# Softmax scaling of all four row blocks on VectorE instead of three shared between VectorE and GpSimd

## The chip, the cores and the metric

The kernel runs on one core of a Trainium2 chip, as one program. The metric is device time in microseconds, from the first to the last instruction of one launch. Of 3 runs of the kernel before, the median is 1939.57 us (1939.19 to 1943.88).

## The reference

Two transformer blocks follow each other on one sequence of 512 tokens and 1024 channels, all in fp32. What matters here are the two dense softmaxes over 512 keys. The first block has a causal attention with 8 heads, the second a window attention and a selected-block attention with 16 heads each; at 512 tokens both of the latter see every earlier key, so that each is a causal softmax too, weighted with a gate per head and row:

```python
sc = jnp.where(k_idx[None, :] <= q_idx[:, None], sc, -jnp.inf)
pr = jax.nn.softmax(sc, axis=-1)                    # first block, 8 heads
...
p_s = jax.nn.softmax(logit_s, axis=-1)              # second block, 16 heads
p_w = jax.nn.softmax(logit_w, axis=-1)              # second block, 16 heads
o = gt[..., 0:1] * o_c + gt[..., 1:2] * o_s + gt[..., 2:3] * o_w
```

That makes 8 softmax tables in the first attention and 32 in the second. The rest are matrix products (input projections, gated feed-forward layers), a depthwise convolution of width 31 beside the first attention, and norms.

## The kernel before

Activations lie transposed, 128 channels to a tile of 512 tokens. Each matrix product is made of three TensorE products of a high and a low part (lines 305 to 307), so every weight and activation is split: ScalarE casts the high part (lines 280 and 286), and VectorE, for some tiles GpSimd, subtracts it for the low part (lines 281 and 287).

A softmax table (`softmax`, from line 484) has four row blocks i = 3, 2, 1, 0 with 512, 384, 256 and 128 allowed keys, side by side in one tile `pw`. For each block TensorE makes the scores (line 500), VectorE adds the bias table and takes the row's minimum into `nm` (line 506), ScalarE takes the exponential and the row sum `rs` (line 508). After two blocks VectorE takes the two reciprocals into `cf` (line 510), and then both blocks are scaled in place by `cf` and by the gate (line 512): a number in the first attention, a column of `gcol` in the second. The pair (3, 2) is scaled by GpSimd, the pair (1, 0) by VectorE. Then `weigh1` and `weigh` transpose the scaled blocks on TensorE (lines 718 and 525), copy or split them (lines 721, 286 and 287) and multiply them with the values (lines 723 and 533); the first transposes of a table with `first` set need all four blocks, those of the other form begin with blocks 2 and 3.

In the first attention VectorE also has the taps of the convolution for two of its four channel tiles (line 610, 512 columns each), GpSimd those of the others (line 608), and GpSimd makes the low parts of keys and queries (lines 287 and 793). In the second attention GpSimd also subtracts the bias table from the mask (`tb`, line 1324), multiplies weights by a norm's gain (line 276) and makes low parts of queries, attention outputs and output weights (lines 287 and 281); VectorE adds the output projection into x (line 1318).

The program is written as one stream. A list scheduler decides at build time in which order the instructions stand on each engine; each engine then goes through its own list in that order, and waits for semaphores where an operand isn't ready. Conv taps and output projections are given a lower priority, so the scheduler uses them as filling.

Of the kernel before, what the change touches and what calls it, by code (L numbers as in the profile page):

```python
# [10 lines left out]
OP = mybir.AluOpType  # L11
# [203 lines left out]
def _body(tc, A, out):  # L215
    nc = tc.nc
    V, S, P, G = nc.vector, nc.scalar, nc.tensor, nc.gpsimd
# [27 lines left out]
    def bank(tag):  # L245
        return ps[0].tile([128, T], FT, name=tag, bufs=banks[tag])
# [238 lines left out]
    def softmax(pl, passes, tab, gate, bufs):  # L485

        nm = pl.tile([128, 4], FT, name="nm", bufs=bufs)
        rs = pl.tile([128, 4], FT, name="rs", bufs=bufs)
        c = pl.tile([128, 4], FT, name="cf", bufs=bufs)
        w = [None] * 4  # L490
        pw = pl.tile([128, 1280], FT, name="pw", bufs=bufs)
        off = 0
        for i in (3, 2, 1, 0):
            n = 128 * (i + 1)
            if i:
                s = bank("s")
                for i_ in (1, 0) if i == 1 else (i,):
                    s_ = s[:, :128 * (i_ + 1)] if i_ else s[:, 256:384]
                    for j, (a, b) in enumerate(passes):
                        P.matmul(s_, a[:, 128 * i_:128 * i_ + 128], b[:, :128 * (i_ + 1)],  # L500
                                 start=j == 0, stop=j == len(passes) - 1)
            else:
                s = s[:, 256:384]
            w[i] = t = pw[:, off:off + n]
            off += n
            V.tensor_tensor_reduce(out=t, in0=s[:, :n], in1=tab[:, 384 - 128 * i:], op0=OP.add, op1=OP.min,  # L506
                                   scale=1.0, scalar=3.0e38, accum_out=nm[:, i:i + 1])
            S.activation(t, t, AF.Exp, bias=nm[:, i:i + 1], scale=-1.0, accum_out=rs[:, i:i + 1])  # L508
            if i % 2 == 0:
                V.reciprocal(c[:, i:i + 2], rs[:, i:i + 2])  # L510
                for k in (i + 1, i):
                    (G if i else V).tensor_scalar(w[k], w[k], c[:, k:k + 1], gate(k), op0=OP.mult, op1=OP.mult)  # L512
        return w

    def weigh(pl, w, vst, o, first, last):
# [181 lines left out]
    for i in range(4):  # L697
        acc = bank("mm")
        for k in range(2):
            s = slice(128 * i, 128 * i + 128)  # L700
            w = slice(512 * k, 512 * k + 512)
# [63 lines left out]
    for hp in range(MH // 2):  # L765
# [15 lines left out]
        for par in range(2):  # L781
            h = 2 * hp + par
            if h == 6:
                conv_norm(0)
            uq = unit(A["w_q_b"][h])
            acc = bank("mm")
            mm(acc, uq, qa)
            qf = at.tile([128, T], FT, name="qf", bufs=1)
            begin = V.tensor_tensor(qf, acc, tq[par], op=OP.mult)
            qh = at.tile([128, T], FR, name="qh", bufs=2)  # L790
            ql = at.tile([128, T], FR, name="ql", bufs=2)
            S.copy(qh, qf)
            (G if h > 1 else V).tensor_tensor(ql, qf, qh, op=OP.subtract)
            with tc.issue_after(begin.ins):
                conv_taps(3, range(SPREAD[h], SPREAD[h + 1]))
            kh, kl = ka[par]
            if h > 5:
                start_out(h - 6)
            w = softmax(at, ((qh, kh), (qh, kl), (ql, kh)), mask, lambda k: 1.0, 3)
            weigh1(w, lambda j: vt[:, j, hp, 64 * par:64 * par + 128], o, par)  # L800
# [91 lines left out]
    for ch in range(3):  # L892
        hid = []
        for f in range(8 * ch, min(8 * ch + 8, FT1)):
# [6 lines left out]
            for k in range(2):  # L901
                V.scalar_tensor_tensor(y, gpad[:, k:k + T], col("ffn_dw_w", 3 * f + k), y,
                                       op0=OP.mult, op1=OP.add)
# [79 lines left out]
    for c in range(KT):  # L983
# [10 lines left out]
        for k in range(2):  # L994
            V.scalar_tensor_tensor(y, gpad[:, k:k + T], col("a_conv_w", 3 * c + k), y,
                                   op0=OP.mult, op1=OP.add)
# [262 lines left out]
    for g in range(4):  # L1259
        d = acc[:, 64 * g:64 * g + 64]  # L1260
        for k in range(2):
            sh, sl = [z[:, k, 128 * g:128 * g + 128] for z in hv]
            w = slice(64 * k, 64 * k + 64)
# [56 lines left out]
    def head(g, j, of):  # L1320
        h = 4 * g + j
        tb = aw.tile([128, T], FT, name="tb", bufs=2)
        nc.sync.dma_start(tb, A["bias"][h])
        G.tensor_tensor(tb, mask, tb, op=OP.subtract)
        o = bank("o")
        place = PLACE[4 * g + j]

        def blocks(n):
            if n == place:
                for e_ in range(2):  # L1330
                    P.matmul(o, vz[:, g, j, :], pcs[g][e_], start=n == 0 and e_ == 0, stop=n == 2 and e_ == 1)

        for b in range(2):
            blocks(b)
            k = kk[g][b]
            w = softmax(aw, ((qs[g][j], k[0]), (qs[g][j], k[1])), tb,
                        lambda i: gcol[:, i, 3 * h + 1 + b:3 * h + 2 + b], 3)
            weigh(aw, w, lambda jt: vt[g][:, jt, b, :], o, b == 0 and place > 0, b == 1 and place < 2)
        blocks(2)
        if h < NH - 1:  # L1340
            fold(aw, o, of, j % 2)
        return o
# [88 lines left out]
```

## Time and profile before

| what | value |
|---|---|
| profiled execution | 1939.04 us, span 1937.2 us |
| TensorE busy | 1858.0 us, 96% of the span |
| VectorE busy | 1295.1 us, 67% |
| ScalarE busy | 956.5 us, 49% |
| GpSimd busy | 412.0 us, 21% |
| TensorE granted clock, mean | 0.983 |

Busy time is a union of the instructions' spans on an engine. Consecutive instructions on VectorE overlap by a few hundredths of a microsecond in the records, so what one costs its queue is the distance from its start to the next start. The first attention's softmaxes run at about 130 to 180 us of the span, the second's at about 1299 to 1540 us; all other stages have no instruction of line 512.

### The profile page before, as it was taken

To read this page: it belongs to the slowest core of one execution; us is meant where nothing else is said; L and a number is where in the kernel's file an instruction comes from. 1 tells how busy PE (TensorE), PEld (TensorE's weight loads), DVE (VectorE), ACT (ScalarE), POOL (GpSimd) and SP (SyncE) were. 2 spreads that over 40 slices of the span, in tenths; PEclk is the share of its full clock that TensorE was granted. 3 is DMA by queue.
4 is the path that set the end of the run, shared out by engine and by line. 5 is a ranking of instruction groups with operands and counts; after the bars stand their busy time and mean duration, and the time that the engine had idled before them with its cause. 6 is when DMAs were issued, how large, how long until landed. Compare 5 with 4: busy or idle time off the path is not lost. (4 is left out here: it accounts for less than half of the span.)

```text
span 1937.2 us, 27654 instructions
## 1 busy us (share of the span) xinstructions
PE 1858.0 (96%) x10198; PEld 1585.8 (82%) x10198; DVE 1295.1 (67%) x2294; ACT 956.5 (49%) x1755; POOL 412.0 (21%) x397
## 2 busy tenths in 40 slices
PE   8989999999999999999999999989999989999997
PEld 6767888888888878878888888778888878898886
DVE  7888566255355864486666666869887977666664
ACT  6686544233234432254444444646665755444443
POOL 2994230000003300010000002336454420000001
PEclk9989989999999999999999999999999989999998
DMA  4221323332322223334455542354232134555542
GB/s 150 81 75 31 100 75 97 98 98 88 98 93 93 77 87 98 118 93 135 130 131 139 142 131 77 111 149 124 78 90 80 36 93 134 148 130 137 136 115 76
DMA packets 82742, 202.11 MB, mean 104 GB/s; under 512 B 9904, under 2 KB 18288, under 8 KB 82608
## 3 DMA queue, kind: packets, MB, share of 16 engines
q1 hardware_dynamic: 77744, 184.88, 31.4%
q0 software_dynamic: 4032, 14.68, 4.5%
q8 instruction: 80, 1.31, 0.3%
q10 hardware_dynamic: 832, 0.79, 0.1%
q14 instruction: 54, 0.44, 0.1%
HBM read 187.73 MB, written 2.10 MB: 98 GB/s over the span
## 5 line engine op out<-in xcount | busy, mean ns | idle before, releaser
L280 ACT CAST whi<-raw 128x512 fp32r<-128x512 f32 (+4 forms) x342 | 260.8, 770 | 454.3 <-PE mm L306 345.8
L281 DVE TENSOR_TENSOR wlo<-raw,whi 128x512 fp32r<-128x512 f32 (+4 forms) x318 | 298.6, 945 | 115.4 <-ACT whi L280 110.7
L305 PE MATMUL mm<-hidh,whi 128*128 128x512 f32 (+1 forms) x794 | 295.3, 379 | 5.6 <-ACT hidh L286 5.0
L306 PE MATMUL mm<-hidl,whi 128*128 128x512 f32 (+1 forms) x794 | 300.4, 379 | 0.0
L307 PE MATMUL mm<-hidh,wlo 128*128 128x512 f32 (+1 forms) x794 | 297.9, 379 | 1.6 <-DVE wlo L281 1.6
L306 PE MATMUL mm<-xgl,whi 128*128 128x512 f32 (+1 forms) x608 | 231.7, 382 | 3.8 <-DVE xgl L290 1.9
L307 PE MATMUL mm<-xgh,wlo 128*128 128x512 f32 (+1 forms) x608 | 232.4, 383 | 0.4 <-DVE wlo L281 0.4
L305 PE MATMUL mm<-xgh,whi 128*128 128x512 f32 (+1 forms) x608 | 231.4, 383 | 0.7 <-ACT whi L280 0.7
L305 PEld LDWEIGHTS mm<-hidh,whi 128*128 128x128 f32 x794 | 148.9, 188 | 32.8 <-ACT hidh L286 5.4
L307 PEld LDWEIGHTS mm<-hidh,wlo 128*128 128x128 f32 x794 | 149.4, 188 | 29.5 <-DVE wlo L281 1.8
L306 PEld LDWEIGHTS mm<-hidl,whi 128*128 128x128 f32 x794 | 149.8, 189 | 27.1 <-DVE hidl L287 0.6
L344 POOL DMA_DIRECT2D raw<-mlp1f x28 | 24.6, 879 | 549.0 <-DMA raw<-mlp1f 273.8
L306 PEld LDWEIGHTS mm<-xgl,whi 128*128 128x128 f32 x608 | 115.4, 190 | 29.0 <-DVE xgl L290 3.0
L307 PEld LDWEIGHTS mm<-xgh,wlo 128*128 128x128 f32 x608 | 115.5, 190 | 22.8 <-DVE wlo L281 0.8
L305 PEld LDWEIGHTS mm<-xgh,whi 128*128 128x128 f32 x608 | 115.2, 190 | 22.9 <-ACT whi L280 1.5
L287 DVE TENSOR_TENSOR wlo<-raw,whi 128x1024 fp32r<-128x1024 f32 x56 | 68.5, 1224 | 92.0 <-ACT whi L286 91.8
L421 POOL TENSOR_TENSOR ssq<-ssq,sq 128x512 f32<-128x512 f32 (+1 forms) x58 | 70.9, 1222 | 246.2 <-ACT sq L418 245.4
L508 ACT ACTIVATE pw<-pw,nm 128x512 f32<-128x512 f32 (+3 forms) x160 | 89.4, 560 | 44.5 <-DVE nm L506 43.3
L286 ACT CAST whi<-raw 128x1024 fp32r<-128x1024 f32 x56 | 58.7, 1051 | 105.1 <-DMA raw<-mlp1f 79.3
L1039 DVE TENSOR_TENSOR x<-mm,x 128x512 f32<-128x512 f32 x116 | 79.7, 688 | 34.6 <-PE mm L307 34.5
L608 POOL TENSOR_TENSOR cy<-cy,tap 128x512 f32<-128x512 f32 x60 | 89.0, 1484 | 16.8 <-ACT tap L607 13.4
L287 DVE TENSOR_TENSOR hidl<-tmp,hidh 128x512 fp32r<-128x512 f32 x94 | 64.5, 686 | 7.2 <-ACT hidh L286 7.1
(868 smaller groups left out, 4656.9 us busy)
## 6 DMA issues: line engine op xcount, KB each, us to landing
raw<-mlp SPq DMA_DIRECT2D x140, 256.0 KB, 2.7
raw<-mlp1f SPq DMA_DIRECT2D x56, 512.0 KB, 3.7
raw<-mlp1f POOLq DMA_DIRECT2D x28, 512.0 KB, 6.4
raw<-a_in SPq DMA_DIRECT2D x24, 512.0 KB, 3.5
raw<-w_gate SPq DMA_DIRECT2D x22, 512.0 KB, 3.5
raw<-w_up SPq DMA_DIRECT2D x22, 512.0 KB, 3.5
raw<-w_down SPq DMA_DIRECT2D x16, 512.0 KB, 3.5
zraw<-mlp1f SPq DMA_DIRECT2D x28, 256.0 KB, 3.5
```

The lines of the kernel that those rows point to most:

```text
L280: S.copy(hi[:, a], raw[:, a])
L281: eng.tensor_tensor(lo[:, a], raw[:, a], hi[:, a], op=OP.subtract)
L286: S.copy(h, src)
L287: (eng or V).tensor_tensor(l, src, h, op=OP.subtract)
L305: P.matmul(acc, hi[:, s], h, start=first and k == 0, stop=False)
L306: P.matmul(acc, hi[:, s], l, start=False, stop=False)
L307: P.matmul(acc, lo[:, s], h, start=False, stop=last and k == n - 1)
L344: nc.gpsimd.dma_start(s, src[:, 2048:3072], accum_op=OP.add)
L421: (V if k >= self.n - 2 or self.fast else G).tensor_tensor(a, a, s[:, ts], op=OP.add)
L508: S.activation(t, t, AF.Exp, bias=nm[:, i:i + 1], scale=-1.0, accum_out=rs[:, i:i + 1])
L608: G.tensor_tensor(conv_y[c], conv_y[c], t, op=OP.add)
L1039: V.tensor_tensor(x[m], acc, x[m], op=OP.add)
```

## The change

In `softmax` the choice of engine at line 512 goes: VectorE scales all four row blocks of every table, GpSimd none.

```diff
             if i % 2 == 0:
                 V.reciprocal(c[:, i:i + 2], rs[:, i:i + 2])
                 for k in (i + 1, i):
-                    (G if i else V).tensor_scalar(w[k], w[k], c[:, k:k + 1], gate(k), op0=OP.mult, op1=OP.mult)
+                    V.tensor_scalar(w[k], w[k], c[:, k:k + 1], gate(k), op0=OP.mult, op1=OP.mult)
```

The scheduler makes a new order of it on every engine, within the two attentions and their borders. On GpSimd, in the first attention, this piece of the difference shows the pairs leaving (`cy_539` is a channel tile of the convolution, `kl` and `ql` are low parts of keys and queries):

```order
 L608 TENSOR_TENSOR cy_539<-cy_539,tap 128x512
 L793 TENSOR_TENSOR ql<-qf,qh 128x512
-L608 TENSOR_TENSOR cy_539<-cy_539,tap 128x512
-L512 TENSOR_SCALAR pw<-pw,cf 128x512
-L512 TENSOR_SCALAR pw<-pw,cf 128x384
-L608 TENSOR_TENSOR cy_539<-cy_539,tap 128x512
+L608 TENSOR_TENSOR cy_539<-cy_539,tap 128x512 x3
 L287 TENSOR_TENSOR kl<-kf,kh 64x512 x2
 L608 TENSOR_TENSOR cy_539<-cy_539,tap 128x512
 L793 TENSOR_TENSOR ql<-qf,qh 128x512
```

What GpSimd keeps closes up: three taps stand there in a row now, with no wait for `cf` between them.

On VectorE, at the same stage, the pair comes in between a tap (line 610) and the key product `kf` with the next block's scores behind it:

```order
 L506 ISA nm 128x1
 L610 SCALAR_TENSOR_TENSOR cy<-cp_106,cols,cy 128x512
+L512 TENSOR_SCALAR pw<-pw,cf 128x512
+L512 TENSOR_SCALAR pw<-pw,cf 128x384
 L770 TENSOR_TENSOR kf<-mm,R 128x512
 L506 ISA pw,nm<-s,mask 128x384
```

Nothing is taken out there; the two instructions stand ahead of work that other engines wait for.

In the second attention, on VectorE, around one value projection (line 1131), the rows before were:

```order
L510 RECIPROCAL cf<-rs 128x2
L512 TENSOR_SCALAR pw<-pw,cf,gcol 128x256
L512 TENSOR_SCALAR pw<-pw,cf,gcol 128x128
L287 TENSOR_TENSOR ptl<-t,pth 128x384
L1131 TENSOR_TENSOR pf<-mm,R 128x512
L281 TENSOR_TENSOR wlo<-raw,whi 128x1024
L287 TENSOR_TENSOR ptl<-t,pth 128x384
```

and they are now:

```order
L1131 TENSOR_TENSOR pf<-mm,R 128x512
L510 RECIPROCAL cf<-rs 128x2
L281 TENSOR_TENSOR wlo<-raw,whi 128x1024
L512 TENSOR_SCALAR pw<-pw,cf,gcol 128x512
L512 TENSOR_SCALAR pw<-pw,cf,gcol 128x384
L510 RECIPROCAL cf<-rs 128x2
L512 TENSOR_SCALAR pw<-pw,cf,gcol 128x256
L512 TENSOR_SCALAR pw<-pw,cf,gcol 128x128
L287 TENSOR_TENSOR ptl<-t,pth 128x384 x2
```

The four scalings of one table stand close together there, and the low parts `ptl` of the transposed blocks, for which TensorE waits, stand behind them.

## Rows read from the trace of the kernel before

**Rows 1.** The head of the page and its lines of 40 equal slices of the span (48.4 us each): busy share of each engine in tenths, and the granted clock of TensorE.

```profile
span 1937.2 us, 27654 instructions
PE 1858.0 (96%) x10198; PEld 1585.8 (82%) x10198; DVE 1295.1 (67%) x2294; ACT 956.5 (49%) x1755; POOL 412.0 (21%) x397
DVE  7888566255355864486666666869887977666664
POOL 2994230000003300010000002336454420000001
```

**Rows 2.** Busy time of each engine in stretches of the first attention, of what follows it, and in four stretches of the second attention; in brackets the instructions.

```profile
core 0: us, PE busy (x) PEld busy (x) DVE busy (x) ACT busy (x) POOL busy (x), PEclk, DMA share, GB/s
130.00:170.00 40.00, 36.85 (x197) 28.75 (x195) 40.00 (x99) 30.70 (x82) 30.11 (x30) 1.00 0.16 44
170.00:180.00 10.00, 10.00 (x55) 7.85 (x55) 7.91 (x29) 5.79 (x19) 2.51 (x4) 1.00 0.01 2
180.00:200.00 20.00, 18.86 (x96) 14.01 (x94) 12.85 (x27) 15.63 (x29) 2.47 (x2) 1.00 0.28 92
...
1299.00:1360.00 61.00, 60.41 (x343) 51.85 (x342) 54.58 (x133) 38.79 (x94) 32.46 (x27) 1.00 0.37 103
1360.00:1420.00 60.00, 58.65 (x336) 49.16 (x335) 54.05 (x163) 43.04 (x121) 30.81 (x34) 1.00 0.28 74
1420.00:1480.00 60.00, 59.18 (x327) 50.63 (x326) 43.37 (x107) 32.88 (x80) 29.66 (x27) 1.00 0.37 104
1480.00:1540.00 60.00, 56.31 (x330) 47.72 (x328) 56.55 (x171) 44.92 (x128) 29.11 (x36) 0.97 0.12 36
sum 241.00, PE 234.54 PEld 199.35 DVE 208.55 ACT 159.63 POOL 122.03; mean PE 58.64 PEld 49.84 DVE 52.14 ACT 39.91 POOL 30.51
```

**Rows 3.** The same four stretches of the second attention, for the instructions of line 512 alone: VectorE's and GpSimd's.

```profile
1299.00:1360.00 61.00, 12.04 (x14) 11.22 (x14) 1.00 0.37 103
1360.00:1420.00 60.00, 11.33 (x20) 14.41 (x20) 1.00 0.28 74
1420.00:1480.00 60.00, 4.26 (x11) 7.42 (x10) 1.00 0.37 104
1480.00:1540.00 60.00, 11.23 (x20) 14.34 (x20) 0.97 0.12 36
```

**Rows 4.** Groups of line 512 by shape, over the whole span: engine, operation, tiles, shapes, count, busy us and mean ns of one, idle time before. Those with `gcol` are of the second attention.

```profile
L512 POOL TENSOR_SCALAR pw<-pw,cf,gcol 128x512 f32<-128x512 f32 x32 | 25.3, 792 | 66.1 <-DVE cf L510 42.8 <-PE s L500 8.9 <-PE t L525 7.3
L512 POOL TENSOR_SCALAR pw<-pw,cf,gcol 128x384 f32<-128x384 f32 x32 | 22.6, 705 | 0.0
L512 DVE TENSOR_SCALAR pw<-pw,cf,gcol 128x256 f32<-128x256 f32 x32 | 23.6, 737 | 0.6
L512 DVE TENSOR_SCALAR pw<-pw,cf,gcol 128x128 f32<-128x128 f32 x32 | 17.9, 558 | 0.0
L512 DVE TENSOR_SCALAR pw<-pw,cf 128x128 f32<-128x128 f32 x8 | 5.8, 728 | 0.0
L512 DVE TENSOR_SCALAR pw<-pw,cf 128x256 f32<-128x256 f32 x8 | 3.9, 489 | 0.0
```

**Rows 5.** Line 512 on VectorE with nothing of GpSimd beside it: one pair of the first attention and one of the second, each first as duration min/median/max, then as it stands in the order of time (start us, us from first start to last end) with the next instruction behind it; then two other scalings of VectorE with 512 columns on 64 partitions, the first with a column as scalar, the second with numbers.

```profile
L512 DVE TENSOR_SCALAR pw<-pw,cf x2: 282/315/348, 174.2 to 174.4; 128x256 f32<-128x256 f32 x1, 128x128 f32<-128x128 f32 x1
162.39 0.54 DVE L512 TENSOR_SCALAR pw<-pw,cf 128x256 f32<-128x256 f32 x2
162.85 0.68 DVE L789 TENSOR_TENSOR qf<-mm,rope 128x512 f32<-128x512 f32 x1
...
L512 DVE TENSOR_SCALAR pw<-pw,cf,gcol x2: 326/360/395, 1529.0 to 1529.3; 128x256 f32<-128x256 f32 x1, 128x128 f32<-128x128 f32 x1
1529.02 0.65 DVE L512 TENSOR_SCALAR pw<-pw,cf,gcol 128x256 f32<-128x256 f32 x2
1529.60 0.40 DVE L506 CUSTOM_DVE_ANT_0 pw<-s,tb 128x256 f32<-128x256 f32 x1
...
L648 DVE TENSOR_SCALAR rope<-posf,cols 64x512 f32<-64x512 f32 x1 | 0.5, 472 | 0.0
L650 DVE TENSOR_SCALAR rn<-rn 64x512 f32<-64x512 f32 x1 | 0.4, 408 | 0.0
```

**Rows 6.** VectorE's pairs of line 512 and GpSimd's instructions that ran at the same time, in order of time (start us, us).

```profile
1390.82 2.64 DVE L512 TENSOR_SCALAR pw<-pw,cf,gcol 128x256 f32<-128x256 f32 x2
1390.72 1.29 POOL L287 TENSOR_TENSOR stl<-pf,sth 128x512 fp32r<-128x512 f32 x1
1392.10 1.28 POOL L1324 TENSOR_TENSOR tb<-mask,tb 128x512 f32<-128x512 f32 x1
...
1501.05 0.67 DVE L512 TENSOR_SCALAR pw<-pw,cf,gcol 128x256 f32<-128x256 f32 x2
1500.46 1.62 POOL L512 TENSOR_SCALAR pw<-pw,cf,gcol 128x512 f32<-128x512 f32 x2 [2.58 <-DVE cf L510]
```

**Rows 7.** GpSimd's other groups, those with two tensors as input: six of the second attention (1299 to 1540 us), then the largest of the first (110 to 180 us), in the columns of rows 4.

```profile
L1324 POOL TENSOR_TENSOR tb<-mask,tb 128x512 f32<-128x512 f32 x14 | 19.2, 1372 | 8.4 <-DMA tb<-bias 8.3
L276 POOL TENSOR_TENSOR raw<-raw,cols 128x1024 f32<-128x1024 f32 x9 | 17.1, 1904 | 11.8 <-DVE nm L506 7.0 <-DMA raw<-w_q 2.3 <-DMA raw<-w_k 1.8
L287 POOL TENSOR_TENSOR stl<-pf,sth 128x512 fp32r<-128x512 f32 x9 | 13.2, 1466 | 12.4 <-ACT sth L286 12.4
L287 POOL TENSOR_TENSOR obl<-of,obh 128x512 fp32r<-128x512 f32 x7 | 9.1, 1295 | 6.6 <-ACT obh L286 6.6
L281 POOL TENSOR_TENSOR wlo<-raw,whi 128x256 fp32r<-128x256 f32 x12 | 8.9, 746 | 8.7 <-ACT whi L280 8.1 <-PE mm L306 0.7
L281 POOL TENSOR_TENSOR wlo<-raw,whi 128x384 fp32r<-128x384 f32 x8 | 8.1, 1018 | 4.1 <-ACT whi L280 3.0 <-PE t L1307 1.1
...
L608 POOL TENSOR_TENSOR cy<-cy,tap 128x512 f32<-128x512 f32 x18 | 25.6, 1421 | 1.9 <-ACT tap L607 1.1
```

**Rows 8.** Who waited for whom, 1299 to 1540 us: the engine and line that waited, for what, us in total, times, longest.

```profile
POOL pw L512 <- DVE cf L510: 42.8, 17, 6.6
PE s L500 <- DVE nm L506: 3.0, 3, 1.7
```

**Rows 9.** The longest pieces of the chain that ended last, 1299 to 1540 us: start us, us, what.

```profile
1390.90 2.57 DVE pw L512 x2
1411.28 2.39 DVE pw L512 x2
```

## The prediction

> **What bounds the kernel now.** I read the page's head and slices first: TensorE is busy for 96% of the span and VectorE for 67% [rows 1]. Read alone, these shares say that VectorE has a third of its time to spare. The slices say otherwise for two places: VectorE stands at 8 tenths in slices 2 to 4 and at 7 to 9 in slices 28 to 32, near 1310 to 1550 us, and GpSimd is busy in the same slices [rows 1]. Only there does line 512 exist, so only they count.
>
> Then the stretches. From 130 to 170 us VectorE is busy for 40.00 of 40.00 us while TensorE is busy for 36.85 [rows 2]: the first attention is bound by VectorE. Behind it VectorE has room, 2.1 us in 170 to 180 and 7.1 us in 180 to 200 [rows 2]. In the second attention VectorE is busy for 208.55 of 241 us and TensorE for 234.54 [rows 2], so both are close to the bound, and which one is ahead changes by stretch: 54.58 of 61, 54.05 of 60, 43.37 of 60 and 56.55 of 60 us of VectorE [rows 2]. That TensorE does wait for VectorE there can be seen in the waits (scores for `nm`, 3.0 us [rows 8]) and in the chain, where two pairs of line 512 on VectorE are the longest pieces of their surroundings, 2.57 and 2.39 us [rows 9].
>
> **What goes and comes.** GpSimd loses 80 scalings: 25.3 + 22.6 us in the second attention [rows 4]. Nothing is gained by that alone, since GpSimd is busy for 122 of 241 us there [rows 2] and its scalings mostly wait themselves (42.8 us for `cf` [rows 8]). VectorE gets the same 80, of 512 and 384 columns. What do they take? The clean pairs of 256 and 128 columns take 348 and 282 ns in the first attention, 395 and 326 ns in the second [rows 5]: 66 to 69 ns for 128 columns more, and a fixed part. The trace shows no such scaling of 512 columns on 128 partitions. From below, nothing excludes that slope, and the nearest rows, 512 columns on 64 partitions in 472 and 408 ns [rows 5], lie on it or under it (395 + 2 x 69 = 533, 348 + 2 x 66 = 480). From above it could cost twice the slope. I take the slope. What the queue pays is start to next start: 0.46 us for a clean pair in the first attention and 0.58 us in the second [rows 5]. The new pair has 512 columns more in sum, four steps of 0.07: 0.74 and 0.86 us.
>
> - First attention: 8 tables x 0.74 = 5.9 us.
> - Second attention: 32 x 0.86 = 27.5 us (36 us from above, with twice the slope).
>
> **Collisions.** Line 512 on VectorE does not take its clean time today: means of 737 and 558 ns in the second attention, 489 and 728 in the first [rows 4]. Over clean that is 32 x (0.342 + 0.232) = 18.4 us and 8 x (0.141 + 0.446) = 4.7 us. The cause shows in pairs of rows: the pair at 1390.82 took 2.64 us in place of 0.65 while GpSimd ran two instructions with two input tensors (lines 287 and 1324), whereas the pair at 1501.05 took 0.67 us although GpSimd's own scalings ran through all of it [rows 6]. So the scalings, which leave, cost VectorE next to nothing, and the two-input instructions, which cost it, stay.
>
> On this a rule of the Trainium skill speaks for the change. Its page "SBUF — State Buffer", section "Who interferes with whom", says that a VectorE instruction in a two-port mode, which a scaling of fp32 in SBUF can be, and any GpSimd instruction exclude each other for the whole instruction. The row at 1501.05 does not agree for GpSimd's scalings, those at 1390 do for its two-input work; by the rule, the leaving scalings would take a part of the collisions along and the sum would be 1948 in place of 1957 us (the second rival has the working).
>
> How much do the new pairs collide? Not at all from below; as much again as the old ones from above (18.4 and 4.7 us). Estimate between them: the six groups of [rows 7] for the second attention make 75.6 us, 31% of the 241 us; a pair that starts there at random loses between half of such an instruction, 0.65, and all of it, 1.3 us: 32 x 0.31 x 0.65 to 1.3 = 6 to 13, I take 9.6 us or 0.3 us a pair. In the first attention the taps alone make 25.6 us [rows 7], so I take nearly all of the upper end: 4.5 us.
>
> **The sum.** First attention: 5.9 + 4.5 = 10.4 us more for an engine that is already full. Taps are filling and can move into the 9.2 us that are idle from 170 to 200 us, but then the convolution's norm is late next, and TensorE, busy for 28.9 of those 30 us [rows 2], has little to overtake with. I take half: **+5 us** (0 to 10).
>
> Second attention, by stretch, with 7, 10, 5 and 10 pairs [rows 3] at 0.86 + 0.30 = 1.16 us: 54.58 + 8.1 = 62.7 for 61 us, 54.05 + 11.6 = 65.7 for 60, 43.37 + 5.8 = 49.2 for 60, 56.55 + 11.6 = 68.2 for 60. The overhang is 1.7 + 5.7 + 0 + 8.2 = 15.6 us if VectorE never waits; in its best stretch now it is busy for 94% [rows 2], which at 94% would make 66.7, 69.9, 60 and 72.5: 28 us. Against that the scheduler can even out: with all idle time pooled, 208.55 + 27.5 + 9.6 = 245.7, an overhang of 4.7 us. I take **+13 us**. Behind the new pairs in VectorE's order stand the score blocks (line 506) and `ptl`, for which TensorE waits, so the overhang lands on TensorE's queue.
>
> Sum: 1939.0 (the profiled execution, 0.5 below the median of 1939.57) + 5 + 13 = **1957 us**.
>
> **The rivals.**
> 1. *VectorE becomes the only bound.* Collisions come to the full upper end (18.4 and 4.7 us), because the GpSimd work that remains closes up and meets four scalings in a row, and VectorE reaches 94%: second attention 208.55 + 27.5 + 18.4 = 254.5, at 94% 270.7, +30; first +5. 1974 us. For it: the chain's two longest pieces are such collisions [rows 9]. Against: the third stretch has 16 us of room. Chance 0.15.
> 2. *The scalings on GpSimd were collisions too.* GpSimd's scalings are 47.9 of its 122 us in the second attention, 39%; were collisions shared out by that, 0.39 x (18.4 + 4.7) = 9 us of VectorE's time would come back: 1948 us. This is where the rule of "SBUF — State Buffer" would lead. Against it the row at 1501.05. Chance 0.12.
> 3. *Idle time hides it.* VectorE's 32.5 idle us in the second attention take the 27.5, the new pairs fall between GpSimd's instructions, and the taps slide behind 170 us: 1939 to 1943, no change. Against: the idle time lies half in one stretch, and 130 to 170 us has none. Chance 0.11.
> 4. *Faster.* A pair on GpSimd takes 0.79 + 0.71 us [rows 4] behind whatever GpSimd has in front, on VectorE 0.86 us; the blocks 3 and 2 are scaled earlier, and GpSimd no longer stands 42.8 us before `cf` with `tb` and low parts queued behind. If lateness of these and not VectorE's load is what makes TensorE wait, up to TensorE's idle time comes back: 6.5 us in 1299 to 1540 and 3.2 us in 130 to 170 [rows 2], 1930 us. It decides if VectorE's new work is less than its idle time at each place. Against: GpSimd's results appear hardly anywhere in TensorE's waits [rows 8]. Chance 0.07.
>
> That the move doesn't happen is excluded by the order of the new kernel.
>
> **How the numbers follow.** My forecast has 0.55, with its own range 1946 to 1967. For 8 in 10 I cut off the faster case, most of the hidden one and the far end of the first rival: 1942 to 1976. A measurement here can tell about 0.3%, 5.8 us, from no change. Slower by more: 0.55 + 0.15 and most of rival 2, less a little of my own case, 0.80. Within: rival 3 and the rest, 0.13. Faster: 0.07.
>
> **What would show it.** VectorE busy for 96% or more in 1300 to 1555 us and full until about 176 us; line 512 on VectorE with 512 columns at 0.53 us where GpSimd is quiet, and with a mean over 0.7; more waits of TensorE for `nm` and `ptl`; TensorE's busy time in the second attention unchanged in sum but spread over some 13 us more. I am wrong if the mean of the old pairs of 256 and 128 columns falls to the clean 395 and 326 ns (then GpSimd's scalings were the cause), if TensorE's waits for VectorE don't grow, or if the two attentions are as long as before.

## The result and the profile after

The changed kernel takes 1948.83 us (median; 1945.64 to 1954.65) against 1939.57 us before; the ratio is 1.0054 [1.0041, 1.0067]. It is slower, by 9.3 us where 17.4 were forecast. The profiled execution after took 1948.7 us, so that its rows stand for the median.

The head of the page after, to be read against [rows 1]:

```profile
span 1946.9 us, 27602 instructions
PE 1860.0 (96%) x10198; PEld 1582.5 (81%) x10198; DVE 1321.4 (68%) x2374; ACT 956.0 (49%) x1755; POOL 353.7 (18%) x317
```

VectorE has 80 instructions more, GpSimd 80 fewer, TensorE as many as before. VectorE's busy time grows by 26.3 us. Where the span grew can be read from three borders that every one of these kernels has: the last product with the values of the first attention (line 723), the first product of the second attention (line 1286) and the last with the low part `ptl` (line 533). The rows give duration min/median/max, then first and last start. Before:

```profile
L723 PE MATMUL o<-pt,vt x64: 272/483/645, 139.1 to 189.6; 128*128 128x512 f32 x16, 128*128 128x384 f32 x16, 128*128 128x256 f32 x16, 128*128 128x128 f32 x16
L1286 PE MATMUL s<-q,kc x32: 388/396/477, 1289.4 to 1476.7; 128*128 128x512 f32 x32
L533 PE MATMUL o<-ptl,vt x128: 272/336/562, 1313.7 to 1549.5; 128*128 128x512 f32 x32, 128*128 128x384 f32 x32, 128*128 128x256 f32 x32, 128*128 128x128 f32 x32
```

After:

```profile
L723 PE MATMUL o<-pt,vt x64: 272/483/697, 141.9 to 195.3; 128*128 128x512 f32 x16, 128*128 128x384 f32 x16, 128*128 128x256 f32 x16, 128*128 128x128 f32 x16
L1286 PE MATMUL s<-q,kc x32: 387/394/475, 1296.1 to 1483.6; 128*128 128x512 f32 x32
L533 PE MATMUL o<-ptl,vt x128: 272/336/614, 1320.1 to 1560.0; 128*128 128x512 f32 x32, 128*128 128x384 f32 x32, 128*128 128x256 f32 x32, 128*128 128x128 f32 x32
```

Up to the end of the first attention 5.7 us are lost (195.3 for 189.6); from there to the second attention 1.0 (1100.8 for 1099.8); in the second attention 3.8 (263.9 for 260.1); behind it 0.8 come back (386.9 for 387.7, to the end of the span). The sum is 9.7, the difference of the two spans. So the first attention lost what was forecast, 5, and the second a third of its forecast, 13.

The stretches of the first attention after, to be read against [rows 2]:

```profile
130.00:170.00 40.00, 33.84 (x173) 25.90 (x172) 40.00 (x92) 27.10 (x70) 21.49 (x17) 1.00 0.15 42
170.00:180.00 10.00, 9.17 (x51) 6.72 (x50) 10.00 (x35) 7.03 (x22) 0.15 (x1) 1.00 0.01 2
```

VectorE, the third pair of numbers, is now full through 170 to 180 us too (10.00 for 7.91), and TensorE has done less by then (173 products for 197 in the first row). That is the stage bound by VectorE, 5 to 6 us longer.

The second attention as one stretch, from its first border to its last, first before and then after (columns as in [rows 2]):

```profile
1289.40:1549.50 260.10, 252.00 (x1421) 213.92 (x1421) 223.20 (x594) 170.50 (x441) 132.12 (x131) 0.99 0.29 83
```

```profile
1296.10:1560.00 263.90, 252.86 (x1421) 213.44 (x1421) 238.00 (x658) 170.71 (x441) 86.26 (x67) 0.99 0.29 82
```

TensorE does the same 1421 products. VectorE has 64 instructions more and only 14.8 us more to do. The groups of line 512 on VectorE after say why, against [rows 4]; the four with `gcol` are the second attention's:

```profile
L512 DVE TENSOR_SCALAR pw<-pw,cf,gcol 128x256 f32<-128x256 f32 x32 | 17.9, 559 | 0.3
L512 DVE TENSOR_SCALAR pw<-pw,cf,gcol 128x384 f32<-128x384 f32 x32 | 17.8, 557 | 0.0
L512 DVE TENSOR_SCALAR pw<-pw,cf,gcol 128x512 f32<-128x512 f32 x32 | 17.5, 546 | 0.4
L512 DVE TENSOR_SCALAR pw<-pw,cf,gcol 128x128 f32<-128x128 f32 x32 | 11.3, 352 | 0.0
...
L512 DVE TENSOR_SCALAR pw<-pw,cf 128x512 f32<-128x512 f32 x8 | 6.3, 782 | 0.0
L512 DVE TENSOR_SCALAR pw<-pw,cf 128x384 f32<-128x384 f32 x8 | 5.3, 664 | 0.0
L512 DVE TENSOR_SCALAR pw<-pw,cf 128x256 f32<-128x256 f32 x8 | 4.5, 557 | 0.0
L512 DVE TENSOR_SCALAR pw<-pw,cf 128x128 f32<-128x128 f32 x8 | 4.4, 548 | 0.0
```

In the second attention the old blocks of 256 and 128 columns, which VectorE scaled all along, fell from 737 and 558 ns to 559 and 352. A new block of 512 columns takes 546 ns, almost the clean 533. Over clean (328, 396, 464 and 532 ns for 128 to 512 columns, by the slope of the prediction) line 512 costs 9.4 us there now, 6.0 of them in the old blocks, where the old blocks alone had 18.3. In the first attention it goes the other way: 4.7 us over clean before, 8.2 after.

What TensorE waited for in the second attention after, longest first:

```profile
PE t L1307 <- DVE tc L1304: 2.2, 1, 2.2
PE s L500 <- DVE nm L506: 1.9, 4, 0.8
PE t L1290 <- DVE tc L1287: 1.4, 1, 1.4
PE o L1331 <- DVE of L541: 1.2, 3, 0.6
PE mm L305 <- DVE x L1318: 1.1, 2, 0.9
PE t L525 <- DVE pw L512: 1.0, 3, 0.5
PE t L525 <- DVE ptl L287: 0.8, 2, 0.5
```

No single wait grew much; `nm` even fell from 3.0 us [rows 8]. The list got longer: all its rows make 7.7 us before and 10.9 after, and this 3.2 is most of the stage's 3.8 us. The chain shows the same drift. Before, it reaches back only to 1386 us, so only the later part of the stage can be compared: first before (1390 to 1549.5 us), then after, from the same distance behind the border on (1396.7 to 1560 us).

```profile
by line: PE o L533 12.5%; PE mm L305 10.3%; PE t L525 10.2%; PE mm L307 9.9%; PE mm L306 9.8%; PE s L500 9.4%; DVE pw L512 5.6%; DVE pw L506 4.5%; PE o L1331 3.7%; DVE ptl L287 3.5%; issue 2.4%; PE s L1286 2.4%; DMA raw<-b_o_last 2.3%; DMA
```

```profile
by line: DVE pw L512 10.5%; PE o L533 9.8%; DVE pw L506 9.4%; PE mm L305 8.4%; PE mm L307 8.3%; DVE ptl L287 8.3%; PE mm L306 8.2%; PE t L525 6.9%; PE s L500 6.5%; DVE x L1318 3.0%; issue 2.6%; PE o L1331 2.5%; DMA raw<-b_o_last 2.1%; DVE o
```

VectorE's scaling, score blocks and low parts went from 5.6, 4.5 and 3.5% of that part to 10.5, 9.4 and 8.3%. For [rows 9] this means that they speak for the stage from 1386 us on only; the longest piece there is a transfer of 3.11 us (`tc` from `biasc`, at 1425.41), ahead of the two pairs.

### The profile page after: what moved, and what is told of

It is laid out like the page before. It is cut to its first block, busy times and chain, and to the rows that moved or that the text cites. A ratio compares the mean times of both kernels' runs of the same rounds, so it can differ in the third digit from the quotient of the medians.

```text
span 1946.9 us, 27602 instructions
## 1 busy us (share of the span) xinstructions
PE 1860.0 (96%) x10198; PEld 1582.5 (81%) x10198; DVE 1321.4 (68%) x2374; ACT 956.0 (49%) x1755; POOL 353.7 (18%) x317
## 3 DMA queue, kind: packets, MB, share of 16 engines
q1 hardware_dynamic: 77744, 184.88, 31.2%
## 4 chain that ended last, share of the span: by engine, by line
PE 75%; DVE 14%; ACT 3%; POOL 3%; issue 2%; DMA 2%; SPq 0%; POOLq 0%; DVEq 0%; ACTq 0%
PE mm L305 18%; PE mm L306 18%; PE mm L307 18%; PE y L371 3%; PE y L372 3%; PE y L370 3%; POOL cy L608 3%; DVE pw L512 2%; PE mm L371 2%; PE mm L370 2%; PE mm L372 2%; DVE pw L506 2%; DVE wlo L281 1%; PE o L533 1%; DVE ptl L287 1%
## 5 line engine op out<-in xcount | busy, mean ns | idle before, releaser
L508 ACT ACTIVATE pw<-pw,nm 128x512 f32<-128x512 f32 (+3 forms) x160 | 89.3, 559 | 49.2 <-DVE nm L506 48.4
```

## Experiments

In the diffs `G` is GpSimd, `V` VectorE, `S` ScalarE; a gate that is a number marks the first attention. Medians, each beside the kernel before on the same chip. A stage is always read between the borders above, in the profiled execution.

How far one execution carries can be read from kernels that go through a stage with the same list of instructions on TensorE, VectorE, ScalarE and GpSimd. The first attention takes 189.6 to 190.1 us in before, second_v, second_g and act32, and 195.3 and 196.0 in after and first_v. The way between the attentions takes 1099.9 to 1104.4 us in before, second_g, act32, before_rev and second_v. The second attention takes 260.1 and 258.4 us in before and first_v, 266.7 and 264.2 in second_v and second_v_tail, 248.3 and 248.2 in second_g and both_g. So the length of the second attention is good to some 2.5 us, and differences of up to 4.5 us between the attentions have another reason than these lists.

**The first attention alone (first_v).**

```diff
-                    (G if i else V).tensor_scalar(...)
+                    (G if i and not isinstance(gate(k), float) else V).tensor_scalar(...)
```

> VectorE scales all four blocks in the first attention alone (8 tables); in the second, blocks 3 and 2 stay on GpSimd. In the changed kernel the first attention ends some 6 us later than before and the second adds some 4 us. If the two parts add up, this one takes +5 to +6 us over the kernel before, about 1945 us, and the old pairs of 256 and 128 columns in the second attention still take means near 737 and 558 ns. If the parts help each other (the first attention's new order shifts what comes later), the time is within 2 us of before or over +8.

1944.74 us against 1939.45, ratio 1.0032 [1.0019, 1.0045]: 5.3 us. Up to the first border 6.4 us are lost (196.0), and the stretches read like those after:

```profile
130.00:170.00 40.00, 34.92 (x171) 26.96 (x171) 40.00 (x95) 27.27 (x70) 21.51 (x18) 0.96 0.15 39
170.00:180.00 10.00, 9.13 (x48) 6.77 (x49) 10.00 (x34) 7.00 (x21) 0.87 (x1) 1.00 0.00 1
```

The second attention, in which GpSimd still scales, takes 258.4 us, and its old blocks have 17.9 us over clean, as before. Between the attentions 2.6 us more are lost, and 1.7 come back in the second, whose list is that of before, and 2.1 behind it, so that 5.2 of the 6.4 are left in the profiled execution. So the first attention's term stands alone and has, within that, the size that was forecast for it.

**The second attention alone (second_v).**

```diff
-                    (G if i else V).tensor_scalar(...)
+                    (G if i and isinstance(gate(k), float) else V).tensor_scalar(...)
```

> VectorE scales all four blocks in the second attention alone (32 tables); the first is as before. Sum of parts: +4 us, about 1943.5 us. Two theories of the collisions: if GpSimd's scalings themselves bring them about (they hold its queue until cf is ready, so that the two-input work behind them starts when VectorE's own pair comes), the pairs of 256 and 128 columns come down to 560 and 350 ns as in the changed kernel, and all excess of line 512 over its clean time to about 9.5 us in place of 18. If the fall was chance of the new order, some other value comes out, 13 to 25 us, and the time rises to +8 or more.

1955.23 us, ratio 1.0083 [1.0067, 1.0099]: half of the change costs 15.8 us, more than the whole. The second attention's stretch:

```profile
1294.00:1560.70 266.70, 254.42 (x1415) 213.76 (x1414) 240.60 (x657) 169.44 (x440) 85.63 (x67) 0.99 0.29 79
```

It is 6.6 us longer with 17.4 us more of VectorE. Line 512 has 11.7 us over clean there (means 569 and 394 ns in the old blocks), between the 9.5 of the first theory and the 13 or more of the second; the time is that of the second (+8 or more), but not through collisions. The first border lies at 189.6 as before. The rest is lost elsewhere: 4.6 us between the attentions, where the lists are those of before, and 7.2 behind the second (394.9 us for 387.7), where the work is that of before but for one output projection (six products, 1415 for 1421 in the row, an estimated 1.4 us, since their starts lie 0.23 us apart before) that slid behind the border. The total therefore can't be read as the price of the moved load, and the next two kernels show how much an order alone can cost.

**The same work in another order (before_rev, after_rev).** The two blocks of a pair are scaled in the other order, in the kernel before and in the one after.

```diff
-                for k in (i + 1, i):
+                for k in (i, i + 1):
```

> The kernel before, with the two blocks of a pair scaled in the other order (2, 3 and 0, 1): the same work on the same engines, but the scheduler makes another order in both attentions (1346 lines of difference on TensorE). If the order alone decides the second attention's length and the stage behind it, the time moves by 3 to 8 us either way and the collisions of VectorE's pairs there (18.4 us now) leave 14 to 22 us. If the load decides, 1937 to 1942 us and collisions of 15 us or more.

> The changed kernel with the two blocks of a pair scaled in the other order: same work, another order on VectorE (1001 lines of difference). If the order decides, the time moves by 3 to 8 us from 1948.8, to either side. If the load decides, 1946 to 1952 us. The collisions of line 512 in the second attention stay below 13 us if they fell because GpSimd's scalings are gone, and go back to some 18 us or more if the fall to 9.5 was chance.

before_rev takes 1948.79 us against 1938.38, 1.0055 [1.004, 1.007]: as much as the whole change, with no instruction moved to another engine. Its attentions cost nothing: the first border at 188.4 (1.2 earlier), the second attention

```profile
1291.50:1551.10 259.60, 251.35 (x1421) 214.06 (x1420) 215.85 (x594) 169.17 (x441) 132.87 (x131) 0.99 0.30 83
```

0.5 us shorter; line 512 has 12.4 us over clean there, below both cases that were named (14 to 22, and 15 or more). It loses 3.3 us between them, where these lists are those of before, and 7.7 behind (395.4 for 387.7). after_rev takes 1950.03 us, 1.0062 [1.0045, 1.0078], and loses 5.0 us at the first border and 5.2 in the second attention (265.3 us, VectorE 240.65), with 387.8 us behind; line 512 has 10.8 us over clean there, below the 13 that were named. So the stages separate two things. What the load costs is inside the attentions and comes again with the order turned. What lies behind them has two lengths, 386 to 388 us or 395 to 397 (392 in act32). Kernels with the same lists there stay within one length (after and after_rev 386.9 and 387.8, second_v and second_g 394.9 and 396.7), so the order seems to choose. The kernels before and after both have the short one, so their difference is not of this kind.

**All scalings on GpSimd, in the second attention or in both (second_g, both_g).** The load goes the other way.

```diff
-                    (G if i else V).tensor_scalar(...)
+                    (G if i or not isinstance(gate(k), float) else V).tensor_scalar(...)   # second_g
+                    G.tensor_scalar(...)                                                   # both_g
```

> GpSimd scales all four blocks in the second attention, VectorE none there (it keeps blocks 1 and 0 of the first). VectorE loses 41.5 us of its 208.6 us in the second attention, GpSimd gains some 31 us and stands at about 153 of 241. If VectorE's load is what lengthens the second attention, TensorE's idle 6.5 us there shrink and the time falls by 3 to 6 us, to 1934 to 1937. If the way of a table through GpSimd (0.79 + 0.71 + some 0.97 us in a row, behind its other work) is what counts, the time stays or grows by up to 10 us.

> GpSimd scales all four blocks in both attentions. The second as in the run before this one. In the first, VectorE, which was full for 40 of 40 us, loses 9.7 us of line 512; GpSimd, busy for 30.1 of 40 us, gains 8. If VectorE's load bounds the first attention, it ends 4 to 8 us earlier and the time is 1928 to 1933. If GpSimd's taps and low parts then come late, the first attention is as long as before or longer, 1936 or more.

1937.49 us, 0.9991 [0.9982, 1.0001], and 1935.99 us, 0.9983 [0.9974, 0.9992]. The second attention of both_g:

```profile
1288.40:1536.60 248.20, 245.91 (x1415) 211.62 (x1414) 190.83 (x529) 168.22 (x440) 165.21 (x195) 1.00 0.31 85
```

It is 11.9 us shorter with 32.4 us less of VectorE, and TensorE is busy for 99% of it; second_g has 248.3. Some 1.4 of the 11.9 us are the output projection that stands behind the border here too. Both give most of it back behind the attention (396.7 and 397.2 us for 387.7), where in both_g TensorE waits for the late output projections among others (3.5 us for the sum of line 1380, 2.5 for that of line 1318); both_g_rev below has these waits too (2.9 and 2.5 us) and the short stage, so they are not the cause.

The first attention gained little: it ends 1.2 us earlier (188.4 for 189.6), where 4 to 8 were expected. TensorE is then nearly full itself, to be read against [rows 2]:

```profile
130.00:170.00 40.00, 38.29 (x203) 29.85 (x201) 39.48 (x100) 32.40 (x86) 36.42 (x42) 1.00 0.16 39
```

So 9.3 us of line 512 given to VectorE there (8.5 before, 17.8 after, from start to next start) cost 5 to 6 us, and the 8.5 taken from it gave 1.2 (2.9 in both_g_rev).

**Neither engine has the pair (act32).** In the second attention ScalarE scales blocks 3 and 2, and without the gate: that factor is left out there, so the operation has one multiplication less.

```diff
+                    if i and not isinstance(gate(k), float):
+                        S.activation(w[k], w[k], AF.Copy, scale=c[:, k:k + 1])
+                    else:
-                    (G if i else V).tensor_scalar(...)
+                        (G if i else V).tensor_scalar(...)
```

> In the second attention ScalarE scales blocks 3 and 2 (by cf alone: their gate is left out), VectorE blocks 1 and 0 as before; the first attention is as before. GpSimd has no scaling there and VectorE no new one. If GpSimd's scalings bring the collisions about by holding back its two-input work until cf comes, the pairs of 256 and 128 columns fall from means of 737 and 558 ns to about 560 and 350. If only the load of two-input work counts, they stay above 680 and 500. ScalarE gains 32 x some 1.2 = 38 us on 160 of 241 us and may get late: 1937 to 1950 us.

1946.97 us, 1.0046 [1.0031, 1.0061]. The old blocks on VectorE (line 515 here):

```profile
L515 DVE TENSOR_SCALAR pw<-pw,cf,gcol 128x256 f32<-128x256 f32 x32 | 17.7, 554 | 0.7
L515 DVE TENSOR_SCALAR pw<-pw,cf,gcol 128x128 f32<-128x128 f32 x32 | 14.2, 445 | 0.0
```

They have 8.8 us over clean in place of 18.3, although VectorE received nothing: the fall comes with the leaving of GpSimd's scalings, and with the new order that this makes. The stage takes 262.8 us all the same, with VectorE 8.6 us lighter and ScalarE busy for 202.1 us where it had 170.5. So a lighter VectorE helps only if what it lost doesn't burden another engine that these chains pass through.

**The collision by itself (micro).** Behind the end of the kernel before stand 48 more VectorE instructions of 512 columns, in six groups: eight scalings alone, beside GpSimd's scalings, beside GpSimd's products of two tensors; then eight instructions with two tensors as input (the first one of another kind, so seven in its rows) beside GpSimd's scalings, beside its products, and alone. GpSimd's groups of products begin with one scaling. The core:

```diff
+    for ph, (dv, gv) in enumerate((("s", None), ("s", "s"), ("s", "t"), ("t", "s"), ("t", "t"), ("t", None))):
+        for i in range(8):
+            if dv == "s":
+                V.tensor_scalar(u, u, z[ph], 1.0, op0=OP.mult, op1=OP.mult)
...
+            if gv == "t":
+                G.tensor_tensor(v, v, b2_, op=OP.mult)
```

> The kernel before with a block of 48 VectorE instructions of 512 columns behind its last stage, in six groups of 8: scalings alone; scalings beside GpSimd scalings; scalings beside GpSimd two-input products; two-input products beside GpSimd scalings; beside GpSimd two-input products; alone. By the prediction: a scaling alone 0.53 us, beside GpSimd's scalings 0.53 to 0.6, beside two-input products of GpSimd 1.2 or more on most of them. By the rule of the page SBUF - State Buffer both kinds hold VectorE off for whole instructions: over 1 us beside either. Time some 45 us over before.

1996.03 us in one execution; only the durations of the added groups count. VectorE's in order of time, start and us, then GpSimd's:

```profile
1937.99 4.14 DVE L1423 TENSOR_SCALAR mbu<-mbu,mbz 128x512 f32<-128x512 f32 x8
1942.36 6.32 DVE L1423 TENSOR_SCALAR mbu<-mbu,mbz 128x512 f32<-128x512 f32 x8
1949.46 9.73 DVE L1423 TENSOR_SCALAR mbu<-mbu,mbz 128x512 f32<-128x512 f32 x8
1962.66 7.65 DVE L1427 TENSOR_TENSOR mbu<-mbu,mba 128x512 f32<-128x512 f32 x7
1971.89 11.07 DVE L1427 TENSOR_TENSOR mbu<-mbu,mba 128x512 f32<-128x512 f32 x7
1986.43 5.05 DVE L1427 TENSOR_TENSOR mbu<-mbu,mba 128x512 f32<-128x512 f32 x7
```

```profile
1942.50 6.72 POOL L1429 TENSOR_SCALAR mbv<-mbv,mbz 128x512 f32<-128x512 f32 x8 [10.38 <-DVE mbz L1432]
1950.58 11.06 POOL L1431 TENSOR_TENSOR mbv<-mbv,mbb 128x512 f32<-128x512 f32 x8
```

A scaling of VectorE takes 0.52 us alone, 0.79 beside a GpSimd scaling and 1.22 beside GpSimd's two-input work. The prediction stood for 0.53 to 0.6 beside the scalings, and that is too little: the scalings that left did cost VectorE something, about 0.27 us each when they run side by side; the two-input work that stayed costs 0.70. In the kernel before 13 old blocks run beside GpSimd's scalings alone: eight lose nothing, like the pair at 1501.05 [rows 6], and five lose 0.22 to 0.39 us.

**The last stage's transposes (before_rev_tail, second_v_tail).** In before_rev and second_v, with the long last stage, TensorE has four transposes of line 465 as its last work; before and after, with the short one, have two. Here the first half's end is given a higher priority, so that its transposes stand earlier.

```diff
-        for i, ts in enumerate(HALVES):
-            finished(r[i], ts)
+        with tc.high_priority(offset=100):
+            finished(r[0], HALVES[0])
+        finished(r[1], HALVES[1])
```

> The kernel before with the blocks of a pair in the other order, and the first half of the final norm given a higher priority, so that on TensorE its two transposes (line 465) stand ahead of the second half's sums (line 436) again, as in the kernel before, and not behind them. Without the second edit it took 1948.8 us, of which the stage from the last attention product to the end made 391.9 us against 383.9 before. If that place at the end makes the difference, 1941 to 1944 us; if the 8 us lie earlier, in the last feed-forward stage, over 1946.

> VectorE scales all four blocks in the second attention alone, as in second_v, with the same higher priority for the first half of the final norm. second_v took 1955.2 us; its part from the last attention product to the end made 391.4 us. If the end's order is what it lost beside the second attention (267.1 against 260.5 us), 1948 to 1951 us remain. If not, over 1953.

1948.94 us, 1.0038 [1.0027, 1.0049], and 1954.77 us, 1.0076 [1.0061, 1.0092]: next to the kernels without the edit (1.0055 and 1.0083) little or nothing. The stage behind the attention stays at 394.8 and 397.1 us. The transposes moved as intended (two are last now), and the time did not follow; both_g_m20 below has them in that place too, and the long stage. Their place is not the cause. What stayed is a wait of 3.5 us of TensorE for the last sum of squares (line 421), which is 1.3 us in the kernel before; it is 2 of the 8 us here, but both_g_m20 waits 1.6 us there and has the long stage.

**Versions that may beat both kernels (both_g_rev, both_g_m20).** both_g with the pair's order turned, and both_g with the output projections nearer to their place in the program.

```diff
-                for k in (i + 1, i):
+                for k in (i, i + 1):                        # both_g_rev
...
-            with tc.high_priority(offset=-100):
+            with tc.high_priority(offset=-20):              # both_g_m20
```

> GpSimd scales all four blocks of every table, with the blocks of a pair in the other order: the same work as both_g (1936.0 us), whose second attention was 12 us shorter than before while its end was 10 us longer. In this order the two transposes of the first half stand ahead of the second half's sums again. If the end's length follows that order, 1927 to 1931 us, which would beat both kernels; if the second attention's 12 us were themselves an accident of the order, 1936 to 1942.

> As both_g, with the fillings of the second attention (projections, queries, keys, values) at priority -20 in place of -100: the same work, a third order, with the first half's transposes ahead of the second half's sums. Load theory: the second attention again 247 to 251 us long, the end 383 to 387, 1927 to 1932 us. Order theory: anything from 1927 to 1945.

both_g_rev takes 1929.79 us against 1940.33, 0.9939 [0.9925, 0.9954], and beats both kernels; both_g_m20 1935.42 us, 0.9973 [0.9962, 0.9984]. The second attention of both_g_rev:

```profile
1286.20:1535.40 249.20, 245.26 (x1415) 211.14 (x1414) 191.21 (x529) 168.20 (x440) 165.90 (x195) 1.00 0.30 85
```

It is 10.9 us shorter than before, and behind it stand 388.1 us, the short length, so that the gain is kept. (The profiled execution was its shortest, 4.6 us below the median.) both_g_m20 has 250.0 and 394.6 us.

## Why the prediction was right, and which term was mis-sized

**Right: the place and the sign.** The two attentions lost 5.7 and 3.8 us; all else together 0.2. VectorE is what TensorE waits for there, by the chain's shares and by second_g and both_g, where a VectorE that is 31.2 and 32.4 us lighter makes the stage 11.8 and 11.9 us shorter.

**Right: the first attention, +5.** Measured 5.7 in the changed kernel, 6.4 in first_v (5.3 between its medians), 5.0 in after_rev. Its parts hold too: VectorE is full until 180 us (176 was named), and the collisions grew by 3.5 us where 4.5 were put in. It holds for load that comes; both_g shows that load taken away there gives little.

**Right: the clean price.** Counted from start to next start and never beyond its own end, line 512 takes 36.9 us of VectorE's queue in the second attention before and 55.0 after: 18.2 more. Adding back the 8.8 us of collisions that went away gives 27.0; 32 x 0.86 = 27.5 was forecast. VectorE's busy time in the stage grew by 14.8, so its other lines make 3.4 us less.

**Near, and in part by luck: how much of the load shows.** The sum took 13 of 27.5 + 9.6 = 37.1 us as visible, 0.35 us for each; the 13 was chosen between 4.7 us (all idle time pooled) and 28, not worked out. Measured in the second attention against the kernel before: 3.8 of 14.8 (0.26), second_v 6.6 of 17.4 (0.38), after_rev 5.2 of 17.4 (0.30), both_g 11.9 of 32.4 in the other direction (0.37). before_rev and act32 lie off this line: 0.5 us shorter with 7.4 us less, and longer with 8.6 us less but a fuller ScalarE. With 2.5 us between two executions of one list, a single rate is good to some 0.15. What sorts the kernels more sharply is TensorE's idle time in the stage, its length less TensorE's busy time: 8.1 to 8.5 us in the four where the engines share the scalings (before, first_v, before_rev, before_rev_tail), 11.0 to 12.3 in the four with all on VectorE, 2.3 to 4.0 in the four with all on GpSimd, and 11.0 in act32.

**Wrong: the collision term of the second attention.** The step read "the scalings, which leave, cost VectorE next to nothing, and the two-input instructions, which cost it, stay", and put 9.6 us for the new pairs on top of the 18.4 of the old ones. Measured are 9.4 us for all four blocks, so 18.6 us of load too much, which at 0.35 is 6.5 us of the 8.3 between the forecast and the profiled execution; the 3.4 us less on VectorE's other lines make another 1.2.

The row it rested on was read without its neighbour. These are GpSimd's rows of the kernel before around the two longest collisions, the pairs of 2.64 us at 1390.82 [rows 6] and of 2.39 us at 1411.28 [rows 9]:

```profile
1389.33 1.42 POOL L512 TENSOR_SCALAR pw<-pw,cf,gcol 128x512 f32<-128x512 f32 x2 [0.34 <-DVE cf L510]
...
1409.90 1.41 POOL L512 TENSOR_SCALAR pw<-pw,cf,gcol 128x512 f32<-128x512 f32 x2 [0.68 <-DVE cf L510]
1411.28 1.28 POOL L1324 TENSOR_TENSOR tb<-mask,tb 128x512 f32<-128x512 f32 x1
```

Both times GpSimd's own pair is released by a `cf`, runs for 1.4 us and is followed at once by two-input work that had queued behind it; and 1.3 to 1.5 us after GpSimd's start VectorE comes to the pair (1, 0). There the wait ties GpSimd's list to VectorE's, and two-input work is let go just when VectorE scales. Going through all 64 old blocks of the kernel before: of the 18.3 us over clean 7.7 fall on two-input work that follows a GpSimd scaling without a gap (under 0.15 us; 4.6 directly, the rest behind other such work), 8.6 on other two-input work, 1.7 on GpSimd's scalings alone, 0.2 on none.

What falls on two-input work in these same old blocks is 16.3 us before and in first_v, 10.4 in before_rev and 13.5 in before_rev_tail, where GpSimd scales, but 5.5 us after, 8.2 in act32, 5.2 in after_rev and 7.2 in second_v, where it doesn't (8.6, 8.2, 9.9 and 10.9 with the new blocks). GpSimd's two-input work fills 31 to 32% of the time in all of them. So the fall goes with the scalings that left, not with less two-input work, and its size hangs on the order too. That the tie is the cause is argued, not shown: work tied in this way makes 38% of the two-input work's time before (28.6 of 75.2 us) and takes 47% of its collisions, little more than its share, and no kernel loosens the tie alone.

**The rivals.** The second gave 1948 us, and 1948.83 was measured. Its mechanism was half right: collisions went with the scalings, but mostly those with two-input work and only 1.7 us of the scalings' own. Its time was right by two errors that cancel: it took 9 us off VectorE where 18.6 were missing, and counted each in full, where the sum shows 0.35. The first rival (VectorE 94% busy or more) didn't come: VectorE is busy for 238.0 of 263.9 us, 90%. The third needed the first attention to hide its part, which it couldn't. The fourth had it the wrong way round; the gain lies in taking all scalings off VectorE.

**What it named as signs.** The mean over 0.7 us for 512 columns was wrong in the second attention (0.546; 0.782 in the first), and so was the 96% of 1300 to 1555 us (232.4 of 255.0 us, 91%). The sign it named against itself, old blocks falling to the clean 395 and 326 ns, came most of the way for 128 columns (352) and half for 256 (559). TensorE's waits grew, though not for `nm`; its busy time is unchanged in sum (252.0 and 252.9 us).

**Left open.** Why the stage behind the second attention has two lengths some 8 us apart. The traces show where it comes up: in its first 55 us. TensorE's transposes of line 465 there, first before, then in before_rev:

```profile
1597.73 0.65 PE L465 MATMUL t<-ident,r 128*128 128x128 f32 x4 [0.68 <-DVE r L454]
1602.68 1.12 PE L465 MATMUL t<-ident,r 128*128 128x128 f32 x4 [3.62 <-DVE r L454]
```

They come 48.2 and 51.6 us behind the border, after a wait of 0.68 and 3.62 us. The wait is 0.7 us in the five kernels with the short stage and in act32, and 2.8 to 3.6 in the seven with the long one. The first 70 us behind the border, before and in before_rev, columns as in [rows 2]:

```profile
1549.50:1619.50 70.00, 59.40 (x337) 52.88 (x336) 54.04 (x105) 40.79 (x78) 11.18 (x13) 0.88 0.39 111
1551.10:1621.10 70.00, 57.02 (x316) 51.05 (x315) 52.39 (x102) 40.90 (x76) 11.63 (x13) 0.80 0.37 102
```

TensorE sits idle for 13.0 us there in before_rev, 10.6 before, and its mean granted clock is 0.80 for 0.88: more of that time is at the lower of the two levels (1.2 GHz), and 21 products fewer are done. Over the whole stage before_rev waits 4.9 us more and is busy for 2.8 us more (365.63 for 362.79). Which instruction's place starts this isn't known.

## What to carry to other kernels

When work leaves an engine, look in its list at what stood behind that work: a wait that releases two engines together also releases whatever is queued behind it, and that may collide in step. Here VectorE's collisions fell by about half when such work left, though that the wait was the reason isn't shown. Price a load between two nearly full engines per microsecond, from a kernel that moves it each way (here 0.26 to 0.38 us of the second attention for 1 us of VectorE, each to some 0.15), and by stage, not by the total. The two ways need not cost the same: in the first attention load given cost 5 to 6 us, and load taken gave 1.2 to 2.9. Look for two executions of one list before a stage's difference is believed. Where a scheduler sets the order, turn the order of two equal instructions once and time it, since here this alone cost as much as the change, most of it far behind the edit.

## What the runs showed of the hardware

A row of VectorE scalings of fp32 slowed beside both kinds of GpSimd work that were run here, but the two do share: with eight scalings on each, VectorE needed 6.32 us (4.14 alone) and GpSimd 6.72 us, at the same time; had each excluded the other, the sixteen would need about 8 x (0.52 + 0.79) = 10.5 us, with GpSimd's mean of 792 ns from [rows 4]. The records show an instruction's span, not for which part of it a port is held. As far as the whole span is meant, on this the rule of the Trainium skill's page "SBUF — State Buffer", section "Who interferes with whom", that one engine fully blocks the other for the whole instruction, does not agree with the run; beside two-input work it is nearer, with 9.73 us for VectorE's eight.

VectorE's products of two tensors suffer as well: 5.05 us for seven alone, 7.65 beside GpSimd's scalings, 11.07 beside GpSimd's products, 0.72, 1.09 and 1.58 us each. So GpSimd's two-input work cost VectorE more than GpSimd's scalings did, whichever of its own two kinds VectorE ran.
